# The sum of squares of a token: two matmuls by ones, a masked product and four sums, or eight matmuls by two columns

## The chip, the cores and the metric

The kernel runs on one core of a Trainium2 chip. The metric is the device time of one execution in microseconds (us); the time of a kernel is the median of several executions. One further execution is recorded by the hardware profiler, and the views shown here are views of that record. Engines are named as the profile names them: PE is TensorE's matmul, PEld its weight load, DVE is VectorE, ACT is ScalarE, POOL is GpSimd, SP is SyncE, which here issues transfers.

## What is computed

The reference is a trunk of two layers over 2048 tokens of width 1024, batch 1. Layer 1 is a gated delta rule with 8 heads, layer 2 a gated linear attention with 4. Both end in the same way: the branch output of a head, 256 values per token, is normalised by its root mean square, multiplied by a gate and projected back.

```python
def gated_rmsnorm(o, w, gate):
    o = o * lax.rsqrt(jnp.mean(o * o, -1, keepdims=True) + RMS_EPS)
    return o * w.astype(jnp.float32) * jax.nn.silu(gate.astype(jnp.float32))

def l2norm(t):
    return t * lax.rsqrt(jnp.sum(t * t, -1, keepdims=True) + L2_EPS)

def gdn_mixer(x, w_in, conv_w, a_log, dt_bias, norm_w, w_out):
    ...
    q = l2norm(qkv[..., :GDN_KEY].reshape(B, T, GDN_HEADS, GDN_DK).astype(f32))
    ...
    o = gated_delta_rule(q, k, v, g, beta)
    o = gated_rmsnorm(o, norm_w, gate)
    return o.reshape(B, T, GDN_VAL).astype(x.dtype) @ w_out

def reference(x, ...):
    for i in range(DEPTH):
        ...
        x = layer_norm(DEEP_ALPHA * x + y, ln_g[i], ln_b[i])
    return x
```

The normalisation is a factor per token and head, so the kernel applies it after the projection: a token's row of the product with the output weights is multiplied by z, the reciprocal root of the token's sum of squares. In layer 1 the sum also takes the squares of the query, because the query's own normalisation is folded into the same factor.

## The kernel before

**Units.** The work is cut into 48 units: a layer, a group of 512 tokens (four groups) and a head; 32 units are of layer 1 and 16 of layer 2. A unit has four parts, in the order of the code: `gemms` (input projections; weights are split into a rounded fp32r part and a remainder, and a product takes three matmuls: high by high, high by low, low by high), `preps` (per chunk of 128 tokens, the matrices of the recurrence), `chains` (the recurrence over the four chunks, state in SBUF, then the sum of squares and z) and `outs` (the projection of the branch output, eight blocks of 128 tokens by 512 columns).

**Two layouts.** In the first unit of each group of layer 1 and in the very last unit (`u.by_tok`), tokens of the branch output lie on partitions, and ScalarE's Square sums a row as it goes. In the other 43 units, channels lie on partitions: the tile `og` is 128 channels x 2 x 512 tokens, so a token's sum runs across partitions. These 43 take the path at the end of `chains` (lines 1072 to 1093). `output` (line 1004) writes the squares into `sq`; VectorE adds the two halves, and in layer 1 the scaled squares of the query; `split` rounds the result to fp32r on ScalarE (tile `oth`) and takes the remainder on VectorE (`otl`). TensorE then multiplies a 128x128 block of ones, held stationary, by each part, 512 columns moving. Every partition of the product holds all 512 sums. The chunk structure turns it back: VectorE multiplies the product, seen as four 128x128 blocks, by the identity (`ident`), and ScalarE copies each block with an accumulated row sum, which leaves the sum of token p of chunk n at partition p, column n of `ssq`. POOL makes z of it with an addition and a power (`rsqrt`). Between the matmuls and the product, the two halves of `og` are split into their own `oth` and `otl` for the projection.

**The projection.** `outs` accumulates six matmuls per block into a PSUM tile (`pso`, one bank) and VectorE adds it into the residual tile `y` with the factor z:

```python
            v.scalar_tensor_tensor(y[:, c], d, u.z[:, n:n + 1], y[:, c], ALU.mult, ALU.add)
```

**The order.** No instruction is issued where the code names it. A `Recorder` notes every operation with its dependencies, a priority (the chain first, then preparation, projection, input projections, layer norm) and an estimated cost; `place` then runs a list scheduler over five queues (VectorE, ScalarE, GpSimd, TensorE, SyncE's transfers) and the program is emitted in that order. In each queue an instruction waits for all before it. Every instruction is emitted from one line, 364, so the profile's rows are told apart by tiles and shapes. The planner's cost of a matmul is in `cost` (lines 189 to 197). PSUM has three banks for the input projections (`psg`), three for all small products (`psc`), one for the state (`psh`) and one for the output projection. The tiles `oth` and `otl` have two buffers each, `sq` one.

Of the kernel before, what the change touches and what calls it, by code (L numbers as in the profile page):

```python
# [10 lines left out]
BF16 = mybir.dt.bfloat16  # L11
AF = mybir.ActivationFunctionType
ALU = mybir.AluOpType
# [3 lines left out]
P = 128  # L17
# [3 lines left out]
TG = 512  # L21
NG = SEQ // TG
NC = TG // P
H1, H2 = 8, 4
DV = 256
# [88 lines left out]
def size_of(shape):  # L114
    n = 1
    for k in shape[1:]:
        n *= k
    return n


class Recorder:
# [61 lines left out]
    def cost(self, op, dst, every):  # L183
        key = op.key
        n = size_of(dst.shape)
        psum = any(isinstance(a, View) and a.of.psum for a in every)
        op.func = None
        if key == "t":
            mov = size_of(every[2].shape) if op.name == "matmul" else size_of(every[1].shape)
            if op.name == "transpose":  # L190
                op.cost = 2 * dst.shape[0] / 2.4 + 4
            elif every[1].dtype == F32:
                op.cost = 2 * max(mov / 1.2 + 3, 0.85 * every[1].shape[-1] + 2)
            else:
                op.cost = mov / 2.25 + 4.5
            op.lag = 210
            op.func = op.name == "matmul" and min(dst.shape[0], every[1].shape[0]) < P
        elif key == "d":
            size = 4 * n * dst.shape[0]
            tag = dst.of.tag if isinstance(dst, View) else ""  # L200
            op.cost, op.lag = 630 if tag == "wc" or tag[:2] == "wk" else 560 if tag == "wraw" else 480, DMA_LAG + size / 170
            if tag == "Arep":
                op.cost, op.lag = 430, REP_LAG
            elif tag in ("y", "woraw"):
                op.lag = 9500
        elif key == "a":
            size = 4 * n * dst.shape[0]
            op.cost, op.lag = 340, DMA_LAG + size / 170 + (2500 if isinstance(every[1], View) and every[1].of.tag == "xraw" else 0)
        elif key == "v":
            n = max(n, max(size_of(a.shape) for a in every))  # L210
            took = (150 if psum else 160) + 1.04 * n
            if op.name in ("tensor_reduce", "copy_predicated", "tensor_tensor_scan"):
                took += 1.0 * n
            if op.name != "tensor_tensor" and any(isinstance(a, (View, bass.AP)) and size_of(a.shape) == 1
                                                  for a in every[1:]):
                took += 62 if psum or n < 512 else 85
            op.cost, op.lag = took - 80, 80 + LAG
        elif key == "s":
            took = (165 if psum else 210) + 0.833 * n
            if any(isinstance(op.kw.get(k), (View, bass.AP)) for k in ("scale", "bias")):  # L220
                took += 100 + 67 * ("scale" in op.kw and "bias" in op.kw)
            if "accum_out" in op.kw:
                took += 190
            if op.name == "activation":
                op.func = "ln" if op.args[2] == AF.Ln else None if op.args[2] in (AF.Copy, AF.Square, AF.Identity,
                                                                                 AF.Abs) else "exp"
            op.cost, op.lag = took - 95, 95 + LAG
        else:
            took = 140 + 2.8 * n if len(every) > 2 else 185 + n
            if op.args[-1] == ALU.pow:  # L230
                took = 450 + 160 * n
            op.cost, op.lag = took - 40, 40 + LAG
# [151 lines left out]
def trunk(ctx, tc, x, xT, w_in1, conv, a_log, dt_bias, nw1, w_out1, w_in2, gk_up, gk_b, nw2, w_out2,  # L384
# [3 lines left out]
    v, s, g = (rec.engine(e, k) for e, k in ((nc.vector, "v"), (nc.scalar, "s"), (nc.gpsimd, "g")))  # L388
# [11 lines left out]
    def T(tag, shape, bufs=1, dt=F32, p=None):  # L400
        p = p or sb
        count[0] += 1
        shape, n = list(shape), size_of(shape)
        if p is dr:
            tag = f"{tag}_{count[0]}"
        if tag not in rec.tags:
            rec.tags[tag] = [p.tile([shape[0], n], dt, tag=f"{tag}_{k}", name=f"{tag}_{k}") for k in range(bufs)]
        slots = rec.tags[tag]
        t = View(Tracked(tag, slots, p is ps, count[0], rec.rank), slots[0][:])
        if len(shape) == 3:  # L410
            t = t.rearrange("p (a b) -> p a b", a=shape[1])
        elif len(shape) == 4:
            t = t.rearrange("p (a b c) -> p a b c", a=shape[1], b=shape[2])
        return t

    def PS(tag, shape):
        t = T("ps" + tag, [P, 512], PS_BUFS[tag], p=ps)
        n = 1
        for k in shape[1:]:
            n *= k  # L420
        a = t[:shape[0], :n]
        if len(shape) == 3:
            a = a.rearrange("p (a b) -> p a b", a=shape[1])
        return a

    def bc(ap, at, n):
        sh = list(ap.shape)
        return ap.unsqueeze(at).broadcast_to(sh[:at] + [n] + sh[at:])
# [3 lines left out]
    def C(k):  # L432
        return cst[:, k, :]

    ident = C(C_ID)
# [6 lines left out]
    ones = T("ones", [P, P], dt=F32R)  # L442
# [39 lines left out]
    def rsqrt(y, a, eps):  # L482
        if eps:
            g.tensor_scalar(y, a, eps, None, ALU.add)
        g.tensor_tensor(y, y if eps else a, mhalf[:, :y.shape[1]], ALU.pow)

    def small(tag, n, bufs=2):
        return T(tag, [P, n], bufs)

    def split(hi, lo, src, eng=None):  # L490
        s.copy(hi, src)
        (eng or v).tensor_tensor(lo, src, hi.bitcast(F32), ALU.subtract)

    def mm(dst, l, r, start=True, stop=True):
        pe.matmul(dst, l, r, start=start, stop=stop)
# [6 lines left out]
    def transposes(dst, src_of, n, w=P, also=()):  # L502
        for i in range(n):
            pe.transpose(dst[:, i, :], src_of(i), cst[:w, C_ID, :w], also=() if i else also)
# [113 lines left out]
    def flat(t):  # L618
        return t.rearrange("p a b -> p (a b)")
# [431 lines left out]
    def chains(u):  # L1051
        rec.rank = R_CHAIN
        chain = gdn_chain if u.kind == 0 else gla_chain
        z, ssq = small("z", NC), small("ssq", NC)
        u.z, u.oT = z, []

        def parts():
            return [[T(k, [P, NC, P], 2, F32R) for k in ("oth", "otl")] for j in range(2)]
        if u.by_tok:
            hl = parts()  # L1060
            u.og = T("og", [P, NC, DV], 1)
            chain(u, ssq)
            if u.kind == 0:
                v.tensor_tensor(ssq[:], ssq[:], u.prep["qn"][:], ALU.add)
            rsqrt(z[:], ssq[:], DV * 1e-6 if u.kind else 0.0)
            for j in range(2):
                d = PS("c", [P, NC, P])
                transposes(d, lambda n: u.og[:, n, j * P:(j + 1) * P], NC)
                split(hl[j][0][:], hl[j][1][:], d)
                u.oT.append(hl[j])  # L1070
            return
        u.og = T("og", [P, 2, TG], 1)
        sq = T("sq", [P, 2, TG])
        chain(u, sq)
        v.tensor_tensor(sq[:, 0], sq[:, 0], sq[:, 1], ALU.add)
        if u.kind == 0:
            s.activation(sq[:, 1], flat(u.kq[:, 1]), AF.Square, scale=Q_NORM ** 0.5)
            v.tensor_tensor(sq[:, 0], sq[:, 0], sq[:, 1], ALU.add)
        sqh, sql = (T(k, [P, TG], 2, F32R) for k in ("oth", "otl"))
        split(sqh[:], sql[:], sq[:, 0])  # L1080
        d = PS("c", [P, TG])
        mm(d, ones[:], sqh[:], True, False)
        mm(d, ones[:], sql[:], False, True)
        hl = parts()
        for j in range(2):
            split(flat(hl[j][0][:]), flat(hl[j][1][:]), u.og[:, j])
            u.oT.append(hl[j])
        v.tensor_tensor(sq[:, 0].rearrange("p (n t) -> p n t", n=NC), d.rearrange("p (n t) -> p n t", n=NC),
                        bc(ident, 1, NC), ALU.mult)
        for n in range(NC):  # L1090
            jk = T("junk", [P, DV], 1, BF16)
            s.activation(jk[:, :P], sq[:, 0, n * P:(n + 1) * P], AF.Copy, accum_out=ssq[:, n:n + 1])
        rsqrt(z[:], ssq[:], DV * 1e-6 if u.kind else Q_NORM * 1e-6)

    def outs(u):
# [74 lines left out]
    for u in units:  # L1170
        rec.unit = u.at
        gemms(u)
        preps(u)
        chains(u)
        outs(u)
# [54 lines left out]
```

## Time and profile before

| what | value |
|---|---|
| median of 3 executions | 3030.2 us (3029.43 to 3033.52) |
| the profiled execution | 3028.51 us, span 3026.3 us |
| mean granted TensorE clock | 0.988 of full speed |
| busy: PE, PEld | 2926.2 us (97%), 2419.0 us (80%) |
| busy: DVE, ACT, POOL | 2201.4 us (73%), 1243.6 us (41%), 499.8 us (17%) |
| moved by DMA | 612.87 MB, 203 GB/s in the mean |

The span runs from the first to the last instruction. A row of a group gives engine, operation, output and inputs by the program's tile names, the shapes, the count, then busy time and the mean duration of one in ns, and behind the second bar the engine's idle time just before them with what ended it. Matmuls overlap each other, so their mean duration is longer than the distance between two. In the timeline a row has its start in us, the time from the first start to the last end, the engine and the group, with the count at the end (x2: two instructions in one row). A matmul of plain fp32 operands is recorded as two passes, one of fp32r operands as one.

### The profile page before, as it was taken

The numbers are of one execution on the slowest core, as the hardware profiler recorded it, in microseconds if no ns is written. First come the engines' busy times: TensorE is split into PE (matmuls) and PEld (weight loads), VectorE is DVE, ScalarE is ACT, GpSimd is POOL, SyncE is SP. The second block draws the span as 40 slices with busy tenths as digits, with TensorE's granted clock in tenths as the row PEclk, the third lists the DMA queues.
The fourth block names the chain that finished last, engine by engine and source line by source line (L and its number), as shares of the span: only waits on it lengthen the run. The fifth ranks groups of instructions, "written<-read, shape, count | busy, mean of one in ns | idle before, by whom it ended". The sixth has DMA issues, their size and how long they took to land. (4 is left out here: it accounts for less than half of the span.)

```text
span 3026.3 us, 48052 instructions
## 1 busy us (share of the span) xinstructions
PE 2926.2 (97%) x16172; PEld 2419.0 (80%) x16172; DVE 2201.4 (73%) x5374; ACT 1243.6 (41%) x3233; POOL 499.8 (17%) x848
## 2 busy tenths in 40 slices
PE   8899999999999999999999999999999999999997
PEld 6677777778877887887888888887787888888886
DVE  6878788797777686668778778557787777755655
ACT  5445554543332455333343344333343344433331
POOL 5432444320100233210000000001010000000000
PEclk9999999999999999999999999999999999999998
DMA  6566777695565658687556665768655565857654
GB/s 193 175 196 203 239 234 241 209 293 159 167 182 178 191 165 269 213 286 224 161 163 182 190 207 179 242 228 244 175 171 176 154 193 176 268 192 236 221 183 143
DMA packets 480615, 612.87 MB, mean 203 GB/s; under 512 B 57280, under 2 KB 407744, under 8 KB 464240
## 3 DMA queue, kind: packets, MB, share of 16 engines
q1 hardware_dynamic: 449456, 589.81, 62.9%
q10 hardware_dynamic: 30912, 20.00, 2.4%
q8 instruction: 127, 2.08, 0.3%
q14 instruction: 120, 0.98, 0.1%
HBM read 480.36 MB, written 129.30 MB: 201 GB/s over the span
## 5 line engine op out<-in xcount | busy, mean ns | idle before, releaser
L364 PE MATMUL psg<-xh,wc 128*128 128x512 f32 x3936 | 1349.5, 409 | 29.0 <-DMA wc<-wk 16.3
L364 PEld LDWEIGHTS psg<-xh,wc 128*128 128x128 f32 x3936 | 740.5, 190 | 195.8 <-DMA wc<-wk 20.6
L364 PE MATMUL psg<-xl,wc 128*128 128x512 f32 x1968 | 805.8, 410 | 0.2
L364 PE MATMUL pso<-wo,oth 128*128 128x512 f32 x1472 | 486.1, 406 | 19.1 <-DVE y L364 17.6
L364 PEld LDWEIGHTS psg<-xl,wc 128*128 128x128 f32 x1968 | 374.4, 190 | 76.4 <-DVE xl L364 1.7
L364 DVE SCALAR_TENSOR_TENSOR y<-pso,z,y 128x512 f32<-128x512 f32 x368 | 274.9, 747 | 148.6 <-PE pso L364 127.6
L364 DVE SCALAR_TENSOR_TENSOR acc<-pb,taps,acc 128x512 f32<-128x512 f32 x384 | 300.3, 785 | 76.5 <-ACT acc L364 69.2
L364 POOL TENSOR_TENSOR wc<-wraw,wc 128x256 fp32r<-128x256 f32 (+1 forms) x336 | 283.3, 859 | 423.5 <-ACT wc L364 360.3
L364 PEld LDWEIGHTS pso<-wo,oth 128*128 128x128 f32 x1472 | 263.9, 189 | 82.8 <-DVE y L364 29.0
L364 PE MATMUL pso<-wo,otl 128*128 128x512 f32 x736 | 295.8, 402 | 0.6 <-DVE otl L364 0.6
L364 PE MATMUL psg<-wc,xh 128*128 128x256 f32 (+1 forms) x1344 | 265.3, 289 | 6.2 <-DMA wc<-wk 4.6
L364 DVE TENSOR_TENSOR Xt<-Arep,X 128x124 f32<-128x124 f32 (+30 forms) x992 | 238.6, 241 | 30.6 <-DMA Arep<-blk 7.5
L364 DVE TENSOR_TENSOR X<-X,Xt 128x124 f32<-128x124 f32 (+30 forms) x992 | 242.6, 245 | 23.9
L364 ACT ACTIVATE th<-psg 128x512 f32<-128x512 f32 (+1 forms) x170 | 95.2, 572 | 334.4 <-PE psg L364 315.4
L364 PEld LDWEIGHTS psg<-wc,xh 128*128 128x128 f32 x1344 | 214.6, 189 | 15.0 <-DMA wc<-wk 4.6
L364 PE MATMUL psg<-wc,xl 128*128 128x256 f32 (+1 forms) x672 | 189.4, 287 | 0.0
L364 ACT CAST wc<-wraw 128x256 fp32r<-128x256 f32 (+1 forms) x336 | 126.0, 405 | 116.2 <-DMA wraw<-in_w_in 99.3
L364 PEld LDWEIGHTS pso<-wo,otl 128*128 128x128 f32 x736 | 139.1, 189 | 30.6 <-DVE otl L364 1.6
L364 POOL TENSOR_SCALAR z<-ssq 128x4 f32<-128x4 f32 x44 | 16.8, 383 | 804.7 <-ACT junk L364 804.2
L364 ACT COPY pb<-psg 128x512 f32<-128x512 f32 x128 | 74.8, 585 | 148.4 <-PE psg L364 145.6
L364 POOL COPY halo<-pb 128x3 f32<-128x3 f32 x128 | 35.2, 275 | 577.6 <-ACT pb L364 576.3
L364 PEld LDWEIGHTS psg<-wc,xl 128*128 128x128 f32 x672 | 126.1, 189 | 2.7
(193 smaller groups left out, 4280.3 us busy)
## 6 DMA issues: line engine op xcount, KB each, us to landing
wc<-wk SPq DMA_DIRECT2D x856, 256.0 KB, 3.8
wo<-wok SPq DMA_DIRECT2D x70, 1024.0 KB, 5.0
wk<-wc SPq DMA_DIRECT2D x272, 256.0 KB, 3.0
wraw<-in_w_in SPq DMA_DIRECT2D x336, 128.0 KB, 3.5
Arep<-blk SPq DMA_DIRECT2D x128, 256.0 KB, 5.4
wok<-wo SPq DMA_DIRECT2D x24, 1024.0 KB, 5.3
wc<-wk SPq DMA_DIRECT2D x80, 272.0 KB, 5.3
Arep<-blkq SPq DMA_DIRECT2D x128, 128.0 KB, 6.4
```

Source lines behind the costliest of these rows:

```text
L364: tc.keep_in_program_order(op.call(*[real(a) for a in op.args], **{k: real(a) for k, a in op.kw.items()}))
```

## The change

The roles of the two operands are exchanged: each 128-token block of the split squares is held stationary, and two columns of the ones move. The product is then already one sum per partition (twice, in two columns). Eight matmuls, two for each chunk, take the place of two; a ScalarE copy of 128x4 from PSUM into `ssq` follows them, recorded ahead of the splits of `og`; the masked product on VectorE and the four accumulating copies on ScalarE are gone. The planner's cost of a matmul that is not plain fp32 gets a floor of 62 ns, which in this kernel only the new matmuls fall under.

```diff
@@ -192,7 +192,7 @@
             elif every[1].dtype == F32:
                 op.cost = 2 * max(mov / 1.2 + 3, 0.85 * every[1].shape[-1] + 2)
             else:
-                op.cost = mov / 2.25 + 4.5
+                op.cost = max(mov / 2.25 + 4.5, 62)
@@ -1078,18 +1078,16 @@
         sqh, sql = (T(k, [P, TG], 2, F32R) for k in ("oth", "otl"))
         split(sqh[:], sql[:], sq[:, 0])
-        d = PS("c", [P, TG])
-        mm(d, ones[:], sqh[:], True, False)
-        mm(d, ones[:], sql[:], False, True)
+        d = PS("c", [P, NC, 2])
+        for n in range(NC):
+            c = slice(n * P, (n + 1) * P)
+            mm(d[:, n], sqh[:, c], ones[:, :2], True, False)
+            mm(d[:, n], sql[:, c], ones[:, :2], False, True)
+        s.copy(ssq[:], d[:, :, 0])
         hl = parts()
         for j in range(2):
             split(flat(hl[j][0][:]), flat(hl[j][1][:]), u.og[:, j])
             u.oT.append(hl[j])
-        v.tensor_tensor(sq[:, 0].rearrange("p (n t) -> p n t", n=NC), d.rearrange("p (n t) -> p n t", n=NC),
-                        bc(ident, 1, NC), ALU.mult)
-        for n in range(NC):
-            jk = T("junk", [P, DV], 1, BF16)
-            s.activation(jk[:, :P], sq[:, 0, n * P:(n + 1) * P], AF.Copy, accum_out=ssq[:, n:n + 1])
         rsqrt(z[:], ssq[:], DV * 1e-6 if u.kind else Q_NORM * 1e-6)
```

## The prediction

> **What bounds the kernel now.** I read the page first: the busy shares and the clock row.
>
> ```profile
> span 3026.3 us, 48052 instructions
> ...
> PE 2926.2 (97%) x16172; PEld 2419.0 (80%) x16172; DVE 2201.4 (73%) x5374; ACT 1243.6 (41%) x3233; POOL 499.8 (17%) x848
> ...
> PEclk9999999999999999999999999999999999999998
> ```
>
> TensorE is busy for 97% of the span at nearly the full clock; VectorE has a quarter of its time free and ScalarE more than half. So work taken from VectorE or ScalarE pays only where TensorE waits for them, and work added to TensorE costs nearly its whole length. How much waiting there is, by halves of the run (columns: stretch, its length, then PE, PEld, DVE, ACT, POOL busy):
>
> ```profile
> 0.00:1500.00 1500.00, 1430.69 (x7640) 1156.14 (x7641) 1143.59 (x2800) 678.97 (x1834) 397.72 (x622) 0.99 0.68 209
> 1500.00:3027.00 1527.00, 1495.50 (x8534) 1262.81 (x8532) 1057.83 (x2574) 564.67 (x1401) 102.04 (x226) 0.99 0.63 196
> ```
>
> In the first half no matmul runs for 69 us, in the second for about 31 (1526.3 - 1495.5). Relief has little to win in the second half. Then the waits: the weight loads' own, and those around the step that changes (who waits, for whom, us in total, times, longest).
>
> ```profile
> PEld pso L364 <- DVE y L364: 29.0, 35, 3.3
> PEld psg L364 <- DMA wc<-wk: 25.2, 16, 5.0
> PEld psc L364 <- ACT W L364: 11.7, 30, 1.0
> PEld psg L364 <- DVE acc L364: 8.9, 11, 1.8
> PEld psg L364 <- ACT acc L364: 6.6, 7, 2.5
> PEld psg L364 <- ACT wc L364: 6.5, 7, 2.3
> ...
> PEld psc L364 <- ACT oth L364: 5.0, 8, 1.7
> ...
> PEld psc L364 <- DVE otl L364: 1.2, 3, 0.6
> ...
> DVE y L364 <- POOL z L364: 12.9, 9, 3.3
> ...
> ACT junk L364 <- DVE sq L364: 43.5, 31, 2.0
> ```
>
> The largest wait that ends at the changed step is the output projection's: its one PSUM bank is read by VectorE's y, and y needs z, the reciprocal root of the sum.
>
> **The change part by part.** It runs in 43 of the 48 units (28 of layer 1, 15 of layer 2). The groups it removes or replaces, and a small copy as the model of the new one:
>
> ```profile
> L364 PE MATMUL psc<-oth,ones 128*128 128x512 f32 x43 | 17.7, 411 | 2.6 <-ACT oth L364 2.6
> ...
> L364 PE MATMUL psc<-otl,ones 128*128 128x512 f32 x43 | 17.9, 417 | 0.3 <-DVE otl L364 0.3
> ...
> L364 DVE TENSOR_TENSOR sq<-psc,cst 128x512 f32<-128x512 f32 x43 | 29.4, 683 | 0.2
> ...
> L364 ACT ACTIVATE junk<-sq 128x128 bf16<-128x128 f32 x172 | 53.1, 309 | 46.4 <-DVE sq L364 43.5 <-ACT junk L364 0.2
> ...
> L364 ACT ACTIVATION_READ_ACCUMULATOR junk<-sq 128x1 f32 x172 | 32.3, 188 | 0.0
> ...
> L364 ACT COPY ba<-psg 128x16 f32<-128x16 f32 x32 | 5.6, 174 | 0.9 <-PE psg L364 0.9
> ```
>
> *TensorE.* A recorded matmul of 512 columns lasts some 400 ns, but they are pipelined; the time one takes from the stream is the distance to the next. The timeline gives it, and the groups nearest to the new form:
>
> ```profile
> 188.44 0.63 PE L364 MATMUL psg<-xh,wc 128*128 128x512 f32 x2
> 188.90 0.40 PE L364 MATMUL psg<-xl,wc 128*128 128x512 f32 x1
> ...
> 1088.80 1.00 PE L364 MATMUL psc<-D 128*128 128x64 f32 x8
> 1089.61 0.48 PE L364 MATMUL psg<-xh,wc 128*128 128x512 f32 x1
> 1089.93 0.40 PE L364 MATMUL psg<-xl,wc 128*128 128x512 f32 x1
> 1090.16 0.62 PE L364 MATMUL psg<-xh,wc 128*128 128x512 f32 x2
> ...
> 44.14 0.30 PEld L364 LDWEIGHTS psc<-lgz,cst 128*128 128x128 f32 x2 [2.63 <-DVE lgz L364]
> 44.36 0.30 PEld L364 LDWEIGHTS psc<-lgz,ones 128*128 128x128 f32 x2
> 44.58 0.30 PEld L364 LDWEIGHTS psg<-xh,wc 128*128 128x128 f32 x2
> 44.92 0.19 PEld L364 LDWEIGHTS psg<-xl,wc 128*128 128x128 f32 x1
> ...
> 115.29 0.59 PE L364 MATMUL psc<-U,D 128*32 128x32 f32 x16 [1.61 <-DVE U L364]
> 115.81 0.50 PE L364 MATMUL psg<-xh,wc 128*128 128x512 f32 x1
> ```
>
> Two 512-column matmuls start at 188.44, the third 0.46 us later: 0.23 each, so the pair with ones costs 0.46 us now. Its successor is eight matmuls whose stationary operand is a full 128x128 block and whose moving operand is two columns; eight weight loads for two. Eight passes with full weights and 64 moving columns start at 1088.80; the next matmul starts 0.81 later and holds its own successor back by 0.32 instead of the 0.23 after it, so the eight took 0.81 + 0.09 = 0.90 us, 0.112 each. With 32 moving columns and full weights the four loads at 44.14 are followed by the next at 44.58: 0.110 each. Halving the moving columns again changed nothing: the load sets the pace. The loads at 44.58 are of the fp32r kind that the new blocks have: two of them last 0.30, one alone 0.19 (the row at 44.92), so they too start 0.11 apart. A load hides behind a 512-column matmul (0.23), but behind a two-column one there is nothing to hide in. So eight cost 0.88 to 0.90 us against 0.46: +0.43 us a unit, times 43 = +18.5 us of TensorE. Bounds: passes with a 32-column stationary block follow each other in 0.52/16 = 0.033 us, which would give 0.26 us for eight, -0.20 us a unit, -8.6 in all. The upper end is 0.112 for each: +18.9. I take 18.5, from the row with the same full 128 columns.
>
> *Order on TensorE.* All eight write one PSUM tile and so go in the recorded order hi, lo, hi, lo. The first needs only the rounded part, the other seven wait for the remainder (VectorE's otl), as the second matmul did before; that wait is 1.2 us in all now, and I leave it. The planner is told 62 ns for each, 0.50 us for eight, so everything it places behind them starts some 0.4 us late: part of the 18.5, not a second cost.
>
> *VectorE* loses 43 products of 683 ns, 29.4 us. *ScalarE* loses 172 sums with their accumulator reads, 53.1 + 32.3 = 85.4 us, and gets 43 copies of 128x4: by the 128x16 row 0.17 each, 7.5 us; net -78. Neither is on the path; what they give is a share of TensorE's waits.
>
> *The new copy is a new wait.* It stands on ScalarE's queue until the eighth matmul, ahead of the two splits of the branch output, weight splits and bank copies. What it replaces there is a wait too: ScalarE stood 43.5 us for the masked product, 31 times. The copy waits for TensorE alone and not for VectorE's backlog, so I cost it at nothing more; if the cover is gone, it is at most TensorE's 0.43 us lateness in each unit, which then delays bank copies by as much: another few us, kept in the range.
>
> *z comes sooner.* From the last matmul to z the path loses 0.68 for the product and four sums with reads (4 x (0.31 + 0.19) = 2.0), and gets a copy of 0.17 and 0.43 of TensorE: about 2.1 us shorter. y stood 12.9 us for z in 9 goes, 1.4 each, so most of this wait can go. Not all of it reached TensorE, and the new order puts y elsewhere. Bounds 0 and -12.9; I take -5. Late next is y behind VectorE's own work.
>
> *Relief.* VectorE is 1.3% lighter, ScalarE 6%. The rows of TensorE waiting for VectorE sum to 39 us, for ScalarE to 30; in proportion 0.5 + 1.8. The removed work came in bursts at the end of the chain, where it stood ahead of bank copies, so I take -4, between 0 and -10.
>
> PSUM banks are held no longer, and POOL's two steps stay. SP issues the same transfers, but the order of all later work, theirs too, is planned anew. TensorE's loads stood 25.2 us for weight chunks; I leave that wait as it is and put a fifth of it, 5 us either way, into the range for the new order.
>
> **The sum** against the profiled execution's own 3028.5 (span 3026.3 and 2.2 around it; the median of the runs, 3030.2, is 1.7 above): 3028.5 + 18.5 - 5 - 4 = 3038.0, on the median's footing 3039.7. I say 3039, +0.3%.
>
> **The rivals.**
>
> *Nothing comes back.* The second half's 31 us of idle speak for it, the y wait against it. Then 3030.2 + 18.5 = 3048.7.
>
> *Faster: the output bank.* The mechanism is the single bank that y empties. If z's earliness takes away the whole 29.0 us that the projection's loads stood for y, the time is 3030.2 + 18.5 - 29.0 = 3019.7; beyond 18.5 us it decides for faster. For it: it is the largest wait of all loads. Against it: y waited for z only 12.9 of those us, the rest for VectorE's queue and its bank. A half of it gives 3034.
>
> *Loads don't bind.* If an fp32r load were much shorter than the rows say and the planner's 62 ns came true, eight would take 0.50 us, +0.04 a unit, +1.6 in all, and with the same 9 us of relief the time is 3030.2 + 1.6 - 9 = 3022.8. Against it stand the loads at 44.58. The Trainium skill (TensorE: Matmul & The Clock Gate, "Weight-path perf modes") says that the fast weight load switches itself on for 128 weights of an input type other than FP32, and fp32r might count as one; by that rule the time would be the one just given. The trace does not bear it out: an fp32r load lasts 0.19 us and the next follows at 0.11, and the plain fp32 loads at 44.14 and 44.36 show the same 0.30 for two.
>
> **How the numbers follow.** The forecast, loads bind and 4 to 14 us return (3034.7 to 3044.7), 0.50; nothing returns 0.14; the output bank gives 14 to 29 us back 0.22; loads don't bind 0.14. About 0.2% (6.1 us) is what a measurement of this kernel can tell from no change: faster is under 3024, slower over 3036. The forecast lies four fifths on the slower side (0.40, same 0.10); nothing returned adds 0.14 slower; the bank 0.07 faster and 0.15 same; cheap loads 0.09 faster and 0.05 same. Sums: faster 0.16, same 0.30, slower 0.54. The range 3020 to 3049 takes in the bank's whole price and most of the full cost, and leaves out the lower end of cheap loads and costs above the full one. The forecast alone: 3035 to 3045.
>
> **What would show it.** In the profile of the changed kernel the group psc<-oth,ones and psc<-otl,ones is 172 and 172 matmuls with two moving columns; a run of eight in the timeline takes 0.8 to 0.9 us up to the next matmul. At 0.5 or less the price of the load is wrong, and with it the sign. DVE busy is down by about 29 us and ACT by about 78. The wait of DVE y for POOL z falls well below 12.9, and PEld pso for DVE y falls by some us. If that wait falls by over 18, or the waits for bank copies (ACT W, ACT acc, DVE acc) fall together by as much, the relief was sized too small; if ACT now stands long for psc at the copy, the cover that I assumed is not there.

## The result and the profile after

The changed kernel takes 3044.1 us in the median (3040.3 to 3048.6) against 3029.8 for the kernel before: ratio 1.0051, interval 1.0035 to 1.0067, +0.5%. Ratios, here and below, are taken from the executions in the fast state and are not the quotients of the medians; two kernels below (3054.3 and 3062.8 us) each had one slow execution, of 5772 and 4943 us, which counts in the median and not in the ratio. The forecast was +0.3% in a range up to 3049. The time lies inside; the experiments below show that the terms of the sum were wrong in size and that about half of the loss is not in the changed operations themselves.

The page of the changed kernel, the lines that answer to those of before:

```profile
span 3038.2 us, 48252 instructions
...
PE 2933.5 (97%) x16430; PEld 2430.2 (80%) x16430; DVE 2176.2 (72%) x5331; ACT 1187.8 (39%) x2932; POOL 507.7 (17%) x848
```

There are 258 more matmuls (43 x 6), DVE is down by 25.2 us (29 were forecast) and ACT by 55.8. ACT was to fall by 78: the forecast added the durations of the sums and of their reads, and these overlap, as the timeline of the kernel before shows (the read starts 0.21 us into a sum of 0.31):

```profile
196.80 0.31 ACT L364 ACTIVATE junk<-sq 128x128 bf16<-128x128 f32 x1 [1.30 <-DVE sq L364]
197.01 0.18 ACT L364 ACTIVATION_READ_ACCUMULATOR junk<-sq 128x1 f32 x1
```

The new groups of the changed kernel, and the first run of them on TensorE in its timeline:

```profile
L364 PE MATMUL psc<-ones,oth 128*128 128x2 f32 x172 | 37.8, 233 | 1.8 <-ACT oth L364 1.7
...
L364 PE MATMUL psc<-ones,otl 128*128 128x2 f32 x172 | 37.2, 236 | 0.1
```

```profile
194.16 0.40 PE L364 MATMUL psg<-xh,wc 128*128 128x512 f32 x1
194.55 0.27 PE L364 MATMUL psc<-ones,oth 128*128 128x2 f32 x1
...
195.91 0.18 PE L364 MATMUL psc<-ones,otl 128*128 128x2 f32 x1
195.96 0.25 PE L364 MATMUL psc<-ones,oth 128*128 128x2 f32 x1
196.07 0.25 PE L364 MATMUL psc<-ones,otl 128*128 128x2 f32 x1
196.18 0.25 PE L364 MATMUL psc<-ones,oth 128*128 128x2 f32 x1
196.29 0.25 PE L364 MATMUL psc<-ones,otl 128*128 128x2 f32 x1
196.40 0.25 PE L364 MATMUL psc<-ones,oth 128*128 128x2 f32 x1
196.51 0.25 PE L364 MATMUL psc<-ones,otl 128*128 128x2 f32 x1
196.63 0.48 PE L364 MATMUL pso<-wo,otl 128*128 128x512 f32 x1
196.94 0.40 PE L364 MATMUL psg<-xl,wc 128*128 128x512 f32 x1
```

A two-column matmul takes 0.11 us of the stream: the starts from 195.96 to 196.51 are 0.11 apart, and the matmul at 196.63 holds its own successor back by 0.31. This is the price that the forecast read from the 64- and 32-column passes. The rule of the Trainium skill that was weighed (TensorE: Matmul & The Clock Gate, "Weight-path perf modes"), a fast load for 128 weights that are not FP32, is not seen at work for fp32r operands here: their loads follow each other at 0.11 us, as those of plain fp32 do.

The waits of the changed kernel that answer to those shown of before:

```profile
ACT oth L364 <- PE psc L364: 56.8, 40, 2.5
...
PEld pso L364 <- DVE y L364: 26.5, 45, 2.1
...
DVE y L364 <- POOL z L364: 15.6, 16, 1.3
```

The wait of y for z, 12.9 us in 9 goes before, is 15.6 in 16. So the wait did not shrink in this order; in the order of before, further down, it did. ScalarE's stand for the masked product (43.5) is gone, and a stand for TensorE has come: 56.8 us, against 13.5 in the kernel before. Little of it is at the copy (2.9 us in 4 goes); most is at a split that writes `oth`. The second split of `og` is often placed in front of the copy, and by the code it takes over the one of the two `oth` buffers that the small matmuls still read.

### The profile page after: what moved, and what is told of

It is laid out like the page before. It is cut to its first block, busy times and chain, and to the rows that moved or that the text cites. A ratio compares the mean times of both kernels' runs of the same rounds, so it can differ in the third digit from the quotient of the medians.

```text
span 3038.2 us, 48252 instructions
## 1 busy us (share of the span) xinstructions
PE 2933.5 (97%) x16430; PEld 2430.2 (80%) x16430; DVE 2176.2 (72%) x5331; ACT 1187.8 (39%) x2932; POOL 507.7 (17%) x848
## 4 chain that ended last, share of the span: by engine, by line
PE 75%; DVE 9%; DMA 8%; issue 3%; SPq 2%; ACT 2%; POOL 1%; POOLq 0%; ACTq 0%; DVEq 0%
PE psg L364 43%; PE pso L364 14%; PE psc L364 13%; PE psh L364 5%; DMA wraw<-in_w_in 3%; DVE X L364 2%; SPq L364 2%; DVE Xt L364 2%; DVE y L364 1%; DMA wc<-wk 1%; DVE acc L364 1%; DMA Arep<-blk 1%; POOL wc L364 1%; DVE D L364 1%; DMA Gb<-gcT 1%
## 5 line engine op out<-in xcount | busy, mean ns | idle before, releaser
L364 PEld LDWEIGHTS pso<-wo,oth 128*128 128x128 f32 x1472 | 262.0, 189 | 75.8 <-DVE y L364 26.5
L364 POOL TENSOR_SCALAR z<-ssq 128x4 f32<-128x4 f32 x44 | 26.2, 595 | 821.9 <-ACT ssq L364 777.6
L364 DVE SCALAR_TENSOR_TENSOR sg<-th,psg 128x512 f32<-128x512 f32 (+1 forms) x106 | 67.0, 633 | 89.7 <-ACT th L364 84.4
```

Of the source, the lines that this page charges most:

```text
L364: tc.keep_in_program_order(op.call(*[real(a) for a in op.args], **{k: real(a) for k, a in op.kw.items()}))
```

## The experiments

Theory 1 is the forecast's: the loss is eight weight loads for two, less a relief of 4 to 9 us. Theory 2 puts it on the new order and the new waits. The first four kernels tell them apart. Ratios are to the kernel before on the same chip.

**Relief alone.** The two 512-column matmuls stay; the product and the sums go.

```diff
-        d = PS("c", [P, NC, 2])
-        for n in range(NC):
...
-        s.copy(ssq[:], d[:, :, 0])
+        d = PS("c", [P, TG])
+        mm(d, ones[:], sqh[:], True, False)
+        mm(d, ones[:], sql[:], False, True)
+        s.copy(ssq[:], d.rearrange("p (n t) -> p n t", n=NC)[:, :, 0])
```

> Leaves out the true sum: the two 512-column matmuls of the kernel before stay, but the masked product and the four sums are gone, and the small copy takes every 128th column, so z is a wrong number. TensorE's work is that of the kernel before (0.46 us a unit), the work of VectorE and ScalarE that of the changed kernel. If the eight weight loads cost the 14 us (theory 1), this is faster than before by what the relief alone is worth: 4 us (changed kernel's +14 against 18.5 of loads) to 9 us (the prediction's term), 3021 to 3026. If the loss lies in the new order or in the new wait of ScalarE on TensorE (theory 2), the loss stays without the loads: 3036 to 3044.

Measured: 3050.4 us, 1.0084 (1.0065 to 1.0103). Slower than before by 25 us without a single added load and with less work on two engines. Theory 1 has no room for this.

**Four loads.** Only the rounded squares are multiplied.

```diff
-            mm(d[:, n], sqh[:, c], ones[:, :2], True, False)
-            mm(d[:, n], sql[:, c], ones[:, :2], False, True)
+            mm(d[:, n], sqh[:, c], ones[:, :2])
```

> Leaves out the remainders: four matmuls by the rounded squares alone; the split that makes the remainder still runs. Four weight loads at 0.111 us are 0.44 us a unit, as much as the two 512-column matmuls before. Theory 1: 4 x 0.111 x 43 = 19 us less than the changed kernel, 3025, and equal to the kernel with the relief alone. Theory 2: the waits and the order are like the changed kernel's, 3038 to 3044.

Measured: 3045.4 us, 1.0057 (1.0044 to 1.0070). Halving the loads of the changed kernel (1.0051) won nothing.

**Sixteen loads.**

```diff
             mm(d[:, n], sqh[:, c], ones[:, :2], True, False)
-            mm(d[:, n], sql[:, c], ones[:, :2], False, True)
+            mm(d[:, n], sql[:, c], ones[:, :2], False, False)
+            mm(d[:, n], sqh[:, c], ones[:, :2], False, False)
+            mm(d[:, n], sql[:, c], ones[:, :2], False, True)
```

> The eight matmuls run twice, so the sum is doubled: sixteen loads. If each load lengthens the run by its whole 0.111 us (theory 1), 8 x 0.111 x 43 = 38 us more than the changed kernel, 3082. If TensorE's waits take up a part, less: with a quarter taken up, 3073. Theory 2: loads hide and the time stays within 10 us of the changed kernel's 3044.

Measured: 3099.9 us, 1.0249 (1.0231 to 1.0268). That is 60 us over the changed kernel's ratio where the loads account for 38. Loads do cost, but these four times do not lie on one line of loads.

**The old operations in another order.** One constant of the planner moves by 2%.

```diff
-            op.lag = 210
+            op.lag = 214
```

> The kernel before with one constant of the planner changed, TensorE's latency from 210 to 214 ns: same instructions, another order. Measures how much a new order alone moves the time. Theory 1: within 6 us of 3030. If order alone makes differences of the size of the change (theory 2), 10 us or more either way is possible.

Measured: 3043.4 us, 1.0051 (1.0039 to 1.0063). The same instructions, planned again, cost as much as the whole change. Theory 1 and the 5 us that the forecast allowed for a new order both fall. In all four kernels an order was drawn anew along with the edit, so none measures its edit alone.

The next kernels therefore hold the order still. The planner works on the operations of before; when the program is written out, chosen operations are replaced in place:

```diff
         for op in self.place():
-            tc.keep_in_program_order(op.call(...))
+            for call, args, kw in self.swap.get(op, [(op.call, op.args, op.kw)]):
+                tc.keep_in_program_order(call(...))
```

**The change in the old order.** `four(t, at)` stands for the small matmuls of the four blocks of `t`, two columns each from column pair `at` of the bank on.

```diff
-        mm(d, ones[:], sqh[:], True, False)
-        mm(d, ones[:], sql[:], False, True)
...
+        mm(d, ones[:], sqh[:])
+        rec.swap[rec.ops[-1]] = four(sqh, 0)
+        mm(d, ones[:], sql[:])
+        rec.swap[rec.ops[-1]] = four(sql, NC)
+        few = eight[:, :NC, 0]
...
                         bc(ident, 1, NC), ALU.mult)
+        rec.swap[rec.ops[-1]] = [(s.engine.copy, (ssq[:], few), {})]
         for n in range(NC):
...
             s.activation(jk[:, :P], sq[:, 0, n * P:(n + 1) * P], AF.Copy, accum_out=ssq[:, n:n + 1])
+            rec.swap[rec.ops[-1]] = []
```

> The change in the order of the kernel before: the planner works on the old operations, and when the program is written out the first matmul by ones is replaced by the four small ones on the rounded part, the second by the four on the remainder, the masked product by ScalarE's small copy, and the four sums by nothing. The remainders' sums are computed and not added. Theory 3 (the order before is a good draw, and what the change itself costs is loads less relief): 18.5 less 0 to 9, so 9 to 18 us above the kernel before. Theory 4 (the +14 is the new order alone, as a new order of the old operations cost 16): within 5 us of the kernel before, or faster.

Measured: 3032.8 us, 1.0026 (1.0016 to 1.0036): +7.9 us (3026.0 x 0.0026). The small matmuls on TensorE in this kernel's timeline:

```profile
192.54 0.61 PE L365 MATMUL psc<-ones,oth 128*128 128x2 f32 x4
193.00 0.69 PE L365 MATMUL psc<-qd,S 128*128 128x128 f32 x4
...
194.00 0.50 PE L365 MATMUL psc<-ones,otl 128*128 128x2 f32 x4
194.36 0.48 PE L365 MATMUL psg<-xh,wc 128*128 128x512 f32 x1
194.68 0.43 PE L365 MATMUL psg<-xl,wc 128*128 128x512 f32 x1
```

Four take 0.46 us up to the next (192.54 to 193.00), and the other four 0.36 with a successor held back by 0.32 instead of 0.23, 0.45 together. So 0.91 us for eight, as counted; what shows of it in the time is less. z does come sooner in this order, and y's wait for it falls from 12.9 us to 3.6; but the weight loads of the projection stand for y as long as before (29.0 there):

```profile
PEld pso L365 <- DVE y L365: 29.2, 39, 3.1
...
DVE y L365 <- POOL z L365: 3.6, 4, 1.2
```

**The relief in the old order.** As above, with the two 512-column matmuls left as they are.

```diff
         mm(d, ones[:], sqh[:], True, False)
         mm(d, ones[:], sql[:], False, True)
+        few = d.rearrange("p (n t) -> p n t", n=NC)[:, :, 0]
...
                         bc(ident, 1, NC), ALU.mult)
+        rec.swap[rec.ops[-1]] = [(s.engine.copy, (ssq[:], few), {})]
         for n in range(NC):
...
             s.activation(jk[:, :P], sq[:, 0, n * P:(n + 1) * P], AF.Copy, accum_out=ssq[:, n:n + 1])
+            rec.swap[rec.ops[-1]] = []
```

> As the kernel in the old order, but with the two 512-column matmuls kept; the copy takes every 128th column, so z is a wrong number. Relief alone, in the old order. Theory 3 and the prediction: 0 to 9 us faster than before. If the new copy's wait on ScalarE costs more than the work that went (a rival), slower than before by up to 5 us. The difference to the kernel with the eight small matmuls in the same order is the price of the loads: 18.5 us by the prediction, near 0 by theory 4.

Measured: 3024.3 us, 1.0000 (0.9989 to 1.0012). Taking the product and the four sums off VectorE and ScalarE is worth nothing, within 3.5 us either way, and with it the earlier z: y's wait for z is 3.6 us here too, and the projection's loads stand 30.9 us for y. The two kernels differ only in their matmuls, so the eight loads are worth the difference, 3032.8 - 3024.3 = 8.5 us (5 to 11 by the spread of the twelve executions of each), where the count says 18.5 to 18.9 (0.43 to 0.44 x 43). The granted clock does not explain the gap: it is 0.990 in the mean of both.

**Two more orders of the new operations.** The first tells the planner the price that the trace shows, the second changes the constant as in the kernel before.

```diff
-                op.cost = max(mov / 2.25 + 4.5, 62)
+                op.cost = max(mov / 2.25 + 4.5, 112)
```

> The changed kernel with the planner told 112 ns for a small matmul instead of 62: the cost that the trace shows, and another order. If the wrong cost is what hurts, 5 us or more faster than the changed kernel; if only the draw of the order matters, anywhere from 3035 to 3060 by the spread of the orders so far, with no side favoured.

Measured: 3054.3 us, 1.0099 (1.0080 to 1.0119). With the price that the trace shows, the order came out worse.

```diff
-            op.lag = 210
+            op.lag = 214
```

> The changed kernel with the planner's latency of TensorE at 214 instead of 210 ns: another order of the same instructions. The kernel before with this edit stands at 3043, so if the change is worth loads less relief in any order (theory 3), 3043 + 9 to 18 = 3052 to 3061; if the change is worth nothing in itself (theory 4), 3035 to 3050.

Measured: 3062.8 us, 1.0111 (1.0086 to 1.0137). With either constant the new operations stand above the old: 1.0051 to 1.0000 at 210, 1.0111 to 1.0051 at 214.

**A third order of the old operations.**

```diff
-            op.lag = 210
+            op.lag = 206
```

> The kernel before with the planner's latency of TensorE at 206 instead of 210 ns: a third order of the old operations. If the order before is a good draw among many, 3033 to 3050; if the 214 order was a bad one and the usual spread is small, within 5 us of 3027.

Measured: 3054.0 us, 1.0085 (1.0068 to 1.0103). Three orders of the old operations stand at 1.0000, 1.0051 and 1.0085, three of the new ones at 1.0051, 1.0099 and 1.0111. The kernel before is the best draw of its three. Where a draw is lost shows in the stretch up to 1500 us: the matmuls issued by then are 7640 in the kernel before. At 214 (first row) and at 206 (second):

```profile
0.00:1500.00 1500.00, 1427.47 (x7608) 1152.15 (x7609) 1149.95 (x2793) 678.91 (x1830) 396.34 (x621) 0.99 0.68 208
```

```profile
0.00:1500.00 1500.00, 1416.37 (x7500) 1146.45 (x7501) 1129.31 (x2777) 670.88 (x1812) 392.34 (x614) 0.98 0.67 207
```

The third order is 140 matmuls behind, and 83 of these have 512 columns (52 of the input projections, 31 of the output projection); at 0.23 us each that is 19 us, most of its 25.7. The second is 32 behind, 15 of them of 512 columns, 3.5 us, and loses the rest later.

A part of such a loss goes with the granted clock. The third order's six executions were granted 0.984 to 0.988 of full speed (median 0.985), the sixteen of the kernel before that were taken beside them 0.988 to 0.993 (0.990). Among those sixteen, 0.001 less clock goes with 2.5 us more time (the slope of a straight line through them), so as an estimate 12 of the 25.7 us go with the clock. The relief alone (0.9865) and the sixteen loads in a free order (0.987) were granted less too, which by the same estimate is 9 of the 25 us of the first and, against the changed kernel's 0.9915, 11 of the 60 us of the second. Whether an order lowers the clock, and by what, was not tried. The changed kernel (0.990 to 0.992) and the kernels in the old order (medians 0.989 to 0.991) stand on about the same clock as the kernel before.

**Sixteen loads in the old order.** The edit is against the change in the old order: each small matmul is issued twice.

```diff
-                    for n in range(NC)]
+                    for n in (*range(NC), *range(NC))]
```

> In the order of the kernel before: as the kernel with eight small matmuls in that order, but each of them is issued twice, sixteen loads; the remainders' sums are not added. The step from two 512-column matmuls to eight small ones added 18.5 us of TensorE by the count and 8.5 us of time (3024.3 to 3032.8). If TensorE's waits take up a fixed half of what is added, eight more loads (0.89 us a unit, 38 us) add 17 to 20 us: +0.8 to 0.9% over before. If the waits had room only for the first ten us and are then used up, the full 38 us come on top: +1.5%.

Measured: 3073.3 us, 1.0155 (1.0137 to 1.0173): +46.9 us, 39.0 more than with eight, where the count says 38.2 (8 x 0.111 x 43). Some ten us of the first step did not reach the end; of the second step nothing was lost. In the timeline eight take 0.91 us up to the next matmul, 0.11 each again.

```profile
195.63 1.05 PE L365 MATMUL psc<-ones,oth 128*128 128x2 f32 x8
196.54 0.69 PE L365 MATMUL psc<-qd,S 128*128 128x128 f32 x4
```

**One 512-column matmul in the old order.** The opposite sign: the remainder is left out.

```diff
         split(sqh[:], sql[:], sq[:, 0])
+        rec.swap[rec.ops[-1]] = []
         d = PS("c", [P, TG])
-        mm(d, ones[:], sqh[:], True, False)
-        mm(d, ones[:], sql[:], False, True)
+        mm(d, ones[:], sqh[:])
+        mm(d, ones[:], sql[:])
+        rec.swap[rec.ops[-1]] = []
```

> The kernel before in its own order with the remainder left out: the split that makes it and the second 512-column matmul by ones are not issued, the masked product and the four sums stay. TensorE has 0.23 us a unit less, 9.9 us in all, VectorE 29.5. If half of a change of TensorE's work shows, as from two matmuls to eight, 4 to 5 us faster than before, and the fastest of all kernels here; if z's or y's waits set the time, no change.

Measured: 3017.3 us, 0.9969 (0.9958 to 0.9979), 9.4 us faster than before and the fastest of all. The 9.9 us of TensorE that it takes away show in full, not by half. It also takes 29.5 us from VectorE; relief of that size was worth nothing in the kernel with the relief in the old order, so I put the gain down to TensorE. That is argued: no run takes the matmul away and leaves the split.

**The old operations in the new order.**

```diff
-        d = PS("c", [P, NC, 2])
+        bank = PS("c", [P, TG])
+        d = bank[:, :2 * NC].rearrange("p (n k) -> p n k", n=NC)
...
             mm(d[:, n], sqh[:, c], ones[:, :2], True, False)
+            rec.swap[rec.ops[-1]] = [] if n else [(pe.engine.matmul, (bank, ones[:], sqh[:]), dict(start=True, stop=False))]
             mm(d[:, n], sql[:, c], ones[:, :2], False, True)
+            rec.swap[rec.ops[-1]] = [] if n else [(pe.engine.matmul, (bank, ones[:], sql[:]), dict(start=False, stop=True))]
         s.copy(ssq[:], d[:, :, 0])
+        jk = rec.tags["junk"][0][:]
+        rec.swap[rec.ops[-1]] = [(v.engine.tensor_tensor, (sq[:, 0].rearrange("p (n t) -> p n t", n=NC),
+                                  bank.rearrange("p (n t) -> p n t", n=NC), bc(ident, 1, NC), ALU.mult), {})] + [
+            (s.engine.activation, (jk[:, :P], sq[:, 0, n * P:(n + 1) * P], AF.Copy),
+             dict(accum_out=ssq[:, n:n + 1])) for n in range(NC)]
```

> The reverse of the kernel in the old order: the planner works on the changed operations, and the old ones are written out in their places: two 512-column matmuls at the places of the first two small ones, the masked product and four sums at the place of the copy. If the +14 of the changed kernel is 8 of loads and the rest the draw of the order (theory 3), this stands 6 to 7 us above before, 3032 to 3036, and the stand of ScalarE behind the masked product may add some us. If the new order costs nothing, 3027.

Measured: 3095.0 us, 1.0230 (1.0210 to 1.0250). Inconclusive for the order. The five longer operations stand where the plan had room for one short copy, so z is late (y's wait for it is 42.5 us, against 15.6 in the changed kernel) and the output bank with it; the plan also frees the tile of squares at the split, earlier than the product reads it, which can make some z other numbers. The row of the projection's wait for y has more than doubled, from 26.5 in the changed kernel:

```profile
PEld pso L365 <- DVE y L365: 63.2, 59, 2.1
```

## Why the prediction was right, and where it was not

- **The price of a small matmul: right.** 0.11 us each, eight at 0.88 to 0.91, the same for 2, 32 and 64 moving columns over a full stationary block.
- **What of the added TensorE time reaches the end: mis-sized.** The step "work added to TensorE costs nearly its whole length" gave 18.5 us; in an unchanged order the runs show 8.5 (5 to 11). It holds for the next eight (39.0 for 38.2) and for 0.23 us a unit taken away (9.4 for 9.9, if TensorE is the reason). Why the first step alone lost ten us on the way is open; the profile of that kernel names no wait that shrank by as much, and its clock was no higher.
- **z comes sooner, -5: the wait went, the gain did not come.** In an unchanged order y's wait for z fell from 12.9 to 3.6 us, as the mechanism said. The step that failed is the next one: the projection's loads stood for y as long as before (29.0 us, then 29.2 and 30.9), and the time did not move. In the changed kernel's own order the wait even rose, to 15.6.
- **Relief, -4: wrong.** The earlier z and the relief together measure 0.0%, within 3.5 us. VectorE's and ScalarE's busy time was no price, as the 97% of TensorE had suggested; a share of TensorE's waits in proportion to the work removed was the mistake. The 39 and 30 us that it was taken from are sums of the rows shown; all rows in which a weight load stands for VectorE or ScalarE sum to 81 and 50.
- **The new wait on ScalarE: in another place.** The forecast looked for it at the copy; in the changed kernel it stands mostly at the split (13.5 to 56.8 us). In the old order the copy stands 12.7 us in 23 goes, and with the relief alone 6.0 in 16.
- **The new order, 5 us either way: far too small.** Three orders of the old operations span 25.7 us. The changed kernel's free order stands 0.25% above its operations in the old order, some 7.5 us.

So the +14 is about 8 of loads and, as what is left over, about 7 that come with the new order, where the forecast had 18.5 less 9. The second part is a difference of two kernels; the run that was to show it by itself was inconclusive. That the forecast of +9 came close was luck: a cost that was too high, relief that did not come and an order that was worse met. The sign from the loads, +0.26% in the old order, is shown.

## What to carry to other kernels

When operands swap roles, count weight loads: a matmul with a full stationary block took 0.11 us however few columns moved. Where a planner writes the order, every edit also draws a new one; measure the draw with a neutral edit of a planner constant, and judge an edit in a frozen order before a difference of half a per cent is explained by it. Look at the granted clock of every execution as well: one order here was granted 0.985 where the kernel before had 0.990. Work taken off VectorE and ScalarE, and a wait that went away off TensorE, were worth nothing that could be measured while TensorE was busy for 97%.

## What the runs showed of the hardware

A small operation of POOL can take three times as long when VectorE works beside it. The addition in z<-ssq takes 128x4 elements. In the kernel before VectorE is idle at 1312.48 us until 1313.87, and the addition takes 0.23 us (POOL's row, then VectorE's next):

```profile
1312.48 0.23 POOL L364 TENSOR_SCALAR z<-ssq 128x4 f32<-128x4 f32 x1 [17.62 <-ACT junk L364]
```

```profile
1313.87 0.75 DVE L364 SCALAR_TENSOR_TENSOR y<-pso,z,y 128x512 f32<-128x512 f32 x1 [2.25 <-POOL z L364]
```

In the changed kernel the earlier z falls beside VectorE's split of `og`, and the same addition takes 0.67 us; it ends 0.09 us after the split:

```profile
1308.95 0.69 DVE L364 TENSOR_TENSOR otl<-og,oth 128x512 fp32r<-128x512 f32 x1 [0.91 <-ACT oth L364]
```

```profile
1309.06 0.67 POOL L364 TENSOR_SCALAR z<-ssq 128x4 f32<-128x4 f32 x1 [14.54 <-ACT ssq L364]
```

It is the rule and not one case: of all additions (before, then changed; least, median and longest in ns) the median rose from 234 to 665. In the changed kernel 33 of the 44 start while a split of `og` runs; all 33 take 0.66 us or more, and 32 of them end 0.09 us after the split. In the kernel before none starts beside such a split; its long ones fall beside other VectorE instructions, and beside several short ones the addition stays at 0.23.

```profile
L364 POOL TENSOR_SCALAR z<-ssq x44: 218/234/999, 200.0 to 2988.4; 128x4 f32<-128x4 f32 x44
```

```profile
L364 POOL TENSOR_SCALAR z<-ssq x44: 229/665/933, 197.0 to 3003.7; 128x4 f32<-128x4 f32 x44
```

The Trainium skill (SBUF — State Buffer, "Who interferes with whom") says that a VectorE instruction with two SBUF inputs contends with a GpSimd instruction that reads SBUF. The split has two such inputs, and the trace agrees: 0.67 us beside it, 0.23 without. What this added 0.4 us costs the kernel was not tried by itself.
